# Gate and up products with x's sums stationary, the weights moving 512 columns wide, and the activations turned by TensorE

## The chip, the cores and the metric

The kernel runs on one core of one Trainium2 chip. The time is device microseconds of one launch; a smaller number is better. All arithmetic is float32: each operand is split into a rounded part (float32r, called hi or wh) and the rest (lo or wl), and one product is three matmuls: hi by hi, hi by lo, lo by hi.

## The reference

Two layers, each with a feed-forward block (FFN), a mixing part (latent attention beside a causal convolution) and a second FFN, on 512 tokens of width 1024. Only the FFNs are changed:

```
def swiglu(x, w_gate, w_up, w_down):
    return (jax.nn.silu(x @ w_gate) * (x @ w_up)) @ w_down
for l in range(DEPTH):                 # 2
    x = x + 0.5 * swiglu(rms_norm(x, ffn1_norm[l]), ...)   # 1024 -> 2816 -> 1024
    ...                                                    # mixing part
    x = x + 0.5 * swiglu(rms_norm(x, ffn2_norm[l]), ...)
    x = rms_norm(x, post_norm[l])
```

There are so four FFNs: FFN1 and FFN2 of layers 0 and 1. The hidden width 2816 is 22 blocks of 128.

## The kernel before

x lies transposed in SBUF: 8 blocks m of 128 features by 512 tokens. The gate and up products of an FFN are computed by a pair of hidden blocks p (128 gate and 128 up columns each, twice).

The first two pairs are plain (`plain`): 8 blocks of features, 512 tokens moving, the weights stationary; this starts before the norm is known, since the norm's factor R is multiplied on afterwards (`plain_out`, L255 to L260). The other nine pairs (`pair`) use a scheme of seven products in place of eight. The product is cut in two along features, tokens and hidden columns; each quarter product has 4 blocks of features, and with the three matmuls and gate beside up that makes 24 matmuls. Sums of the weights' quarters (`s1` to `s4`, L336 to L339) are made on VectorE for each pair, sums of x's quarters (`operands`: `b11`, `b21`, `b22`, `t1` to `t4`) once for an FFN. In these products the weights are stationary and half of the tokens, 256 columns, move. `product` issues the matmuls, `split_into` (L223, L225) splits each weight tile on ScalarE (hi) and VectorE (lo).

The down products (`group`, L140 to L142, updates of x at L399) follow in four chunks of hidden blocks (`CHUNKS`). TensorE's results lie as hidden columns by tokens, as the down product needs its moving operand.

The norm: `Stats` squares x on ScalarE (L172), adds up on GpSimd (L173) and sums over features by a matmul with ones (L178); GpSimd takes the power (L158); `spread` (L192, L196) makes of the factor for each token a tile R with all partitions alike.

The order on each engine is set by a list scheduler: an instruction written earlier goes first if its operands and buffers are ready by the scheduler's own estimate, else a later one goes ahead. Buffers come from pools: 7 PSUM banks (`ps`), 41 slots `r` for split x and activations, 4 each for weights `wh` and `wl`, 3 `raw`, 5 `fr`.

Of the kernel before, what the change touches and what calls it, by code (L numbers as in the profile page):

```python
# [15 lines left out]
P = 128  # L16
# [19 lines left out]
RING = 41  # L36
CHUNKS = ((0, 2), (2, 5), (5, 8), (8, 11))
# [30 lines left out]
def encoder_kernel(ctx: ExitStack, tc: tile.TileContext, xT, consts, vecs, rgain, wgu1, wd1,  # L68
# [56 lines left out]
    def load_w(src, w, kind=""):  # L125
        raw = wpool.tile([P, WC], FP, tag="raw", name=nm("raw"), bufs=3)
        nc.sync.dma_start(out=raw[:, :w], in_=src)
# [100 lines left out]
    def ffn(l, gx, norm, wgu, wd, gain, done, w0=None):  # L228
        with tc.tile_pool(name="f", bufs=4) as fpool:
            ffn_body(fpool, l, gx, norm, wgu, wd, gain, done, w0)  # L230

    def ffn_body(fpool, l, gx, norm, wgu, wd, gain, done, w0):

        def wide(tag="e"):
            return fpool.tile([P, 2, S], FP, tag=tag, name=nm(tag))

        def raw(q, p):
            t = fpool.tile([P, WC], FP, tag="fr", name=nm("fr"), bufs=5)
            nc.sync.dma_start(out=t, in_=wgu[l, p, q])
            return t

        def plain(os, ws, ks):
            for gu, o in enumerate(os):
                for k in ks:
                    w = ws[k % 2]
                    c = slice(gu * 512 + k // 2 * P, gu * 512 + (k // 2 + 1) * P)  # L250
                    mm3(o, w[0][:, c], w[1][:, c], gx[k][0], gx[k][1], k == 0, k == KD - 1)

        def plain_out(os, R):
            t = tmp()
            V.tensor_tensor(t, os[0], R, ALU.mult)  # L255
            s = tmp()
            A.activation(s, t, AF.Silu)
            u = tmp()
            V.tensor_tensor(u, os[1], R, ALU.mult)
            V.tensor_tensor(u, u, s, ALU.mult)  # L260
            return split(u)

        X = {n: [] for n in ("b11", "b21", "b22", "t1", "t2", "t3", "t4")}

        def operands(R):

            es, od = [], []
            for i in range(2):
                e, o = wide(), wide()
                for j in range(2):  # L270
                    for par, t in ((0, e), (1, o)):
                        m = 4 * i + 2 * j + par
                        V.scalar_tensor_tensor(t[:, j], x[:, m, :], gain[:, m:m + 1], R, ALU.mult, ALU.mult)
                        yield
                es.append(e)
                od.append(o)
            yield "x"

            def halved(src):
                hi, lo = slot(FR), slot(FR)  # L280
                h3, l3 = (v.rearrange("p (j t) -> p j t", j=2) for v in (hi, lo))
                A.copy(h3, src)
                V.tensor_tensor(l3, src, h3.bitcast(FP), ALU.subtract)  # L283
                return hi, lo

            def diff(a, b, op=ALU.subtract):
                t = tmp().rearrange("p (j t) -> p j t", j=2)
                V.tensor_tensor(t, a, b, op)  # L288
                return t
            for n in ("b11", "b21"):  # L290
                for i in range(2):
                    X[n].append(halved((es if n == "b11" else od)[i][:, :, 0:HS]))
                    yield
            for i in range(2):
                b11, b12, b21, b22 = (v[i][:, :, h * HS:(h + 1) * HS] for v in (es, od) for h in range(2))
                t3 = diff(b12, b22)
                yield
                t2 = diff(t3, b11)
                yield
                X["t2"].append(halved(t2))  # L300
                yield
                X["t3"].append(halved(t3))
                yield
                t1 = diff(b11, b12)
                yield
                X["t1"].append(halved(t1))
                yield
                t4 = diff(b21, t2, ALU.add)
                yield
                X["t4"].append(halved(t4))  # L310
                yield
                X["b22"].append(halved(b22))
                yield

        def product(o, w, n, start, stop):
            for gu in range(2):
                for k in range(4):
                    hi, lo = X[n][k // 2]
                    t = slice(k % 2 * HS, (k % 2 + 1) * HS)
                    c = slice(gu * 512 + k * P, gu * 512 + (k + 1) * P)  # L320
                    mm3(o[:, gu * HS:(gu + 1) * HS], w[0][:, c], w[1][:, c], hi[:, t], lo[:, t],
                        start and gu == 0 and k == 0, stop and k == 3, True)

        def copied(o, src):
            A.copy(o, src)
            return o

        def pair(p):

            a11, a12, a21, a22 = (raw(q, p) for q in range(4))  # L330
            s3 = wpool.tile([P, WC], FP, tag="raw", name=nm("raw"), bufs=3)
            bx, by, bz = bank(), bank(), bank()
            product(bx, split_into("a11", a11), "b11", True, True)
# [603 lines left out]
```

## Time and profile before

| what | value |
|---|---|
| median of 3 runs | 1858.15 us (1855.42 to 1858.24) |
| span of the profiled execution | 1857.6 us |
| TensorE matmul busy | 1816.5 us (98%) |
| TensorE weight load busy | 1623.6 us (87%) |
| VectorE busy | 1353.9 us (73%) |
| ScalarE busy | 935.7 us (50%) |
| GpSimd busy | 341.5 us (18%) |
| bytes moved by DMA | 175.72 MB, mean 95 GB/s |

The profiled execution has no time of its own beside its span; the span is 0.55 us under the median of the runs. Busy time of matmuls is of modelled, overlapping records: what one matmul takes of TensorE is the distance of its start from the next one's start. The same holds for VectorE, where each instruction's record reaches some 0.08 us into the next one.

### The profile page before, as it was taken

The numbers are of one execution on the slowest core, as the hardware profiler recorded it, in microseconds if no ns is written. First come the engines' busy times: TensorE is split into PE (matmuls) and PEld (weight loads), VectorE is DVE, ScalarE is ACT, GpSimd is POOL, SyncE is SP. The second block draws the span as 40 slices with busy tenths as digits, with TensorE's granted clock in tenths as the row PEclk, the third lists the DMA queues.
The fourth block names the chain that finished last, engine by engine and source line by source line (L and its number), as shares of the span: only waits on it lengthen the run. The fifth ranks groups of instructions, "written<-read, shape, count | busy, mean of one in ns | idle before, by whom it ended". The sixth has DMA issues, their size and how long they took to land.

```text
span 1857.6 us, 27862 instructions
## 1 busy us (share of the span) xinstructions
PE 1816.5 (98%) x11240; PEld 1623.6 (87%) x11240; DVE 1353.9 (73%) x1761; ACT 935.7 (50%) x1467; POOL 341.5 (18%) x242
## 2 busy tenths in 40 slices
PE   7999999999899999999999999999999999999997
PEld 6898989888688898989888999898978788989895
DVE  5985858678855985858679767675989569767674
ACT  4453535457944453535634535354679435535351
POOL 3000000238924000000310000002589310000002
PEclk9999999999999999999999999999999999999998
DMA  6142422424213142423512414123250322424221
GB/s 217 41 142 69 135 68 91 122 74 125 46 58 110 39 140 77 128 77 94 165 54 63 150 55 148 57 87 114 78 148 1 108 80 63 142 63 143 63 86 63
DMA packets 55569, 175.72 MB, mean 95 GB/s; under 512 B 6160, under 2 KB 6544, under 8 KB 55440
## 3 DMA queue, kind: packets, MB, share of 16 engines
q1 hardware_dynamic: 53856, 169.37, 29.3%
q0 software_dynamic: 1152, 4.19, 1.3%
q8 instruction: 88, 1.44, 0.3%
q10 hardware_dynamic: 432, 0.38, 0.1%
q14 instruction: 41, 0.34, 0.1%
HBM read 171.82 MB, written 2.10 MB: 94 GB/s over the span
## 4 chain that ended last, share of the span: by engine, by line
PE 82%; DVE 7%; POOL 4%; ACT 4%; issue 3%; DMA 0%; POOLq 0%; ACTq 0%; DVEq 0%
PE ps L140 26%; PE ps L142 26%; PE ps L141 25%; PE ps L664 2%; PE ps L630 1%; ACT pr L707 1%; POOL y L711 1%; DVE wl L135 1%; POOL acc L173 1%; DVE r L283 1%; PE ps L651 1%; DVE cv L703 1%; DVE t L288 1%; POOL sck L158 1%; ACT wh L129 1%
## 5 line engine op out<-in xcount | busy, mean ns | idle before, releaser
L141 PE MATMUL ps<-r,wh 128*128 128x256 f32 (+1 forms) x3280 | 1060.7, 325 | 2.3 <-DVE r L153 2.2
L140 PE MATMUL ps<-r,wh 128*128 128x256 f32 (+1 forms) x3280 | 1053.7, 328 | 8.9 <-ACT wh L129 7.9
L142 PE MATMUL ps<-r,wl 128*128 128x256 f32 (+1 forms) x3280 | 1052.7, 325 | 3.9 <-DVE wl L135 1.9
L140 PEld LDWEIGHTS ps<-r,wh 128*128 128x128 f32 x3280 | 621.4, 191 | 64.8 <-ACT wh L129 8.7
L141 PEld LDWEIGHTS ps<-r,wh 128*128 128x128 f32 x3280 | 625.8, 191 | 55.1 <-DVE r L153 3.2
L142 PEld LDWEIGHTS ps<-r,wl 128*128 128x128 f32 x3280 | 622.2, 191 | 56.8 <-DVE wl L135 4.4
L223 ACT CAST wh<-fr 128x1024 fp32r<-128x1024 f32 x216 | 226.9, 1051 | 318.1 <-PE ps L141 233.0
L129 ACT CAST wh<-raw 128x768 fp32r<-128x768 f32 (+4 forms) x214 | 187.7, 883 | 337.5 <-PE ps L141 170.0
L173 POOL TENSOR_TENSOR acc<-acc,t 128x512 f32<-128x512 f32 x52 | 89.4, 1725 | 1308.5 <-ACT t L172 1307.4
L225 DVE TENSOR_TENSOR wl<-fr,wh 128x1024 fp32r<-128x1024 f32 x216 | 263.8, 1222 | 79.6 <-ACT wh L223 76.6
L135 DVE TENSOR_TENSOR wl<-raw,wh 128x768 fp32r<-128x768 f32 (+4 forms) x198 | 209.5, 1063 | 125.9 <-ACT wh L129 124.5
L399 DVE SCALAR_TENSOR_TENSOR x<-ps,x 128x512 f32<-128x512 f32 x128 | 87.6, 687 | 119.1 <-PE ps L142 119.1
L711 POOL TENSOR_TENSOR y<-y,pr 128x509 f32<-128x509 f32 (+15 forms) x120 | 157.5, 1313 | 51.9 <-ACT pr L707 44.6
L703 DVE SCALAR_TENSOR_TENSOR cv<-r,vec,cv 128x511 f32<-128x511 f32 (+14 forms) x120 | 87.7, 731 | 3.1 <-ACT cv L699 1.7
L707 ACT ACTIVATE pr<-r,vec 128x511 f32<-128x511 f32 (+14 forms) x120 | 83.5, 722 | 8.2 <-POOL y L711 8.0
L223 ACT CAST wh<-raw 128x1024 fp32r<-128x1024 f32 x36 | 37.7, 1047 | 70.3 <-PE ps L141 70.3
L146 ACT CAST r<-t 128x512 fp32r<-128x512 f32 x96 | 55.7, 620 | 33.5 <-DVE t L260 20.6
L147 DVE TENSOR_TENSOR r<-t,r 128x512 fp32r<-128x512 f32 x96 | 64.7, 686 | 10.2 <-ACT r L146 10.2
L225 DVE TENSOR_TENSOR wl<-raw,wh 128x1024 fp32r<-128x1024 f32 x36 | 44.1, 1225 | 30.9 <-ACT wh L223 30.9
L630 PE MATMUL ps<-r,r 96*128 96x384 f32 (+3 forms) x128 | 47.8, 492 | 8.6 <-ACT r L609 4.4
L336 DVE TENSOR_TENSOR raw<-fr,fr 128x1024 f32<-128x1024 f32 x36 | 44.0, 1223 | 12.9 <-DMA fr<-in_wgu 12.9
L153 DVE SCALAR_TENSOR_TENSOR r<-x,vec,r 128x512 fp32r<-128x512 f32 x40 | 45.9, 1148 | 10.2 <-ACT r L152 10.2
(165 smaller groups left out, 1596.4 us busy)
## 6 DMA issues: line engine op xcount, KB each, us to landing
fr<-in_wgu SPq DMA_DIRECT2D x144, 512.0 KB, 3.6
raw<-in_wd SPq DMA_DIRECT2D x96, 384.0 KB, 3.1
raw<-in_wgu SPq DMA_DIRECT2D x32, 512.0 KB, 3.5
raw<-in_wd SPq DMA_DIRECT2D x32, 256.0 KB, 2.6
raw<-in_wcv SPq DMA_DIRECT2D x16, 512.0 KB, 3.6
raw<-in_wout SPq DMA_DIRECT2D x16, 512.0 KB, 4.5
wl<-in_wout POOLq DMA_DIRECT2D x8, 512.0 KB, 6.7
raw<-in_wql SPq DMA_DIRECT2D x6, 512.0 KB, 3.5
```

The costliest lines, as they stand in the source:

```text
L129: A.copy(hi[:, :w], raw[:, :w])
L135: (G if kind in POOLW.split() else V).tensor_tensor(lo[:, :w], raw[:, :w], hi[:, :w].bitcast(FP), ALU.subtract)
L140: T.matmul(o, lh, rh, start=first, stop=False, skip_group_check=free)
L141: T.matmul(o, lh, rl, start=False, stop=False, skip_group_check=free)
L142: T.matmul(o, ll, rh, start=False, stop=last, skip_group_check=free)
L173: (eng or (V if last else G)).tensor_tensor(self.acc, self.acc, sq, ALU.add)
L223: A.copy(hi[:, :w], src[:, :w])
L225: V.tensor_tensor(lo[:, :w], src[:, :w], hi[:, :w].bitcast(FP), ALU.subtract)
L399: V.scalar_tensor_tensor(x[:, m, :], pd, 0.5, x[:, m, :], ALU.mult, ALU.add)
L703: V.scalar_tensor_tensor(acc[:, s:], u[c][:, :S - s], tap(k), acc[:, s:], ALU.mult, ALU.add)
L707: A.activation(pr[:, s:], u[c][:, :S - s], AF.Copy, scale=tap(k))
L711: order["conv"] = G.tensor_tensor(acc[:, s:], acc[:, s:], pr[:, s:], ALU.add).ins
```

## The change

All 22 hidden blocks now go by the scheme of seven products, in six units of 4, 4, 4, 4, 4 and 2 blocks. In a product a 128-token slice of x's sum is stationary and the weights move, 512 columns wide (gate and up of 4 half blocks), in the last unit 256. The result has tokens on partitions. So the norm's factor is a number for each partition (`gated`, no R is needed in an FFN), and the activations are turned by TensorE (`turned`: 4 transposes of 128 by 128 into a bank) before they are split and used by the down products. x's sums are made without the norm, from x times the gain: `block(m)` makes `b11`, `b21` and `b22` as each block of x is finished, and `sums` makes `t1` to `t4` during the first unit, called by `advance`. The down products of unit u are issued between the products of unit u+1 (`down`, two feature blocks for each load of weights); those of the last two units come after all products. At the start of the program x's blocks are loaded in the order 0, 2, 4, 6, 1, 3, 5, 7 among the first weight tiles. After the second FFN of layer 0, x is no longer scaled in place by ScalarE: `post` multiplies gain and factor together on VectorE. Pools: 9 `fr` buffers, 40 slots; the scratch of GpSimd's DMAs is set to 4096 bytes.

```
+UNITS = (4, 4, 4, 4, 4, 2)
...
+    class Operands:
...
+        def block(self, m):
+            g, q = self.g[:, m:m + 1], m // 2
+            if m % 2:
+                hi, lo = split_scaled(x[:, m, :], g)
+                for n, c in (("b21", slice(0, HS)), ("b22", slice(HS, S))):
+                    self.k[n][q] = hi[:, c], lo[:, c]
+                return
...
+            A.activation(hi, x[:, m, 0:HS], AF.Copy, scale=g)
+            V.scalar_tensor_tensor(lo, x[:, m, 0:HS], g, hi.bitcast(FP), ALU.mult, ALU.subtract)
+            self.k["b11"][q] = hi, lo
...
+        def scaled(self, i, par, half, b, op):
+            out = slot()
+            for j in range(2):
+                m, c = 4 * i + 2 * j + par, slice(j * HS, (j + 1) * HS)
+                V.scalar_tensor_tensor(out[:, c], x[:, m, half * HS:(half + 1) * HS], self.g[:, m:m + 1],
+                                       b[:, c], ALU.mult, op)
+            return out
...
+        def product(o, ts, n, start, stop):
+            w = [split_into("q", t) for t in ts]
+            kn = 4 // len(w)
+            N = WC // kn
+            order = [(j, k) for j in range(2) for k in range(4)]
...
+            for j, k in order:
+                hi, lo = ops.k[n][k]
+                t = slice(j * P, (j + 1) * P)
+                c = slice(k % kn * N, (k % kn + 1) * N)
+                mm3(o[j][:, :N], hi[:, t], lo[:, t], w[k // kn][0][:, c], w[k // kn][1][:, c],
+                    start and k == 0, stop and k == 3, True)
...
+        def gated(t, src, out, N):
+            h = N // 2
+            for j in range(2):
+                r = rt[0][:, 2 * t + j:2 * t + j + 1]
+                A.activation(out[j][:, :h], src[j][:, :h], AF.Silu, scale=r)
+                V.scalar_tensor_tensor(out[j][:, :h], src[j][:, h:N], r, out[j][:, :h], ALU.mult, ALU.mult)
+            return out
...
+        def turned(vs, N, act):
+            for b in range(2):
+                for i in range(N // 2 // P):
+                    ps = bank()
+                    for t in range(2):
+                        for j in range(2):
+                            T.transpose(ps[:, (2 * t + j) * P:(2 * t + j + 1) * P],
+                                        vs[b][t][j][:, i * P:(i + 1) * P], ident)
+                    act.append(split(ps))
...
+        def unit(u, between):
+            a11, a12, a21, a22 = (quarter(u, q) for q in range(4))
...
+            product(bx, a11, "b11", True, True)
+            a = sides(copied(bx, N))
+            between(0)
+            product(by, a12, "b21", True, True)
+            if first:
+                ops.advance(6)
+            add(s3, a11, a21)
+            add(a21, a21, a22)
+            add(a11, a11, a21)
+            between(1)
+            if first:
+                rt.append(norm())
+            join(a, a, by, ALU.add, N)
+            gated(0, a, a, N)
+            product(bx, a11, "t2", False, True)
...
+            product(bx, a12, "b22", False, True)
...
+        for ms in ((0, 1, 2), (3,), (4,), (5,), (6,), (7,)):
+            ws = [load_w(wd[l, m, :, f0:f0 + n * P], n * P) for m in ms]
+            pds = [bank() for _ in ms]
+            for pd, w in zip(pds, ws):
+                group(pd, w, acts, range(n0), n)
+            if ms[0] == 0:
+                turned(vs, UNITS[-1] * P, acts)
+            for m, pd, w in zip(ms, pds, ws):
+                group(pd, w, acts, range(n0, n), n)
+                update(m, pd)
+                done(m)
```

In `unit`, `between(0)` is where the turned activations of the unit before are written, `between(1)` to `between(4)` where two feature blocks each of its down products are; the products with `t3`, `t1` and `t4` left out here follow the one with `t2` in the same way. In the changed kernel the lines are others: L146 to L148 are the three matmuls, L366 the transposes, L231 `split_into`'s lo, L323 the weights' sums, L268 `scaled`, L159 `split_scaled`'s lo, L179 the norm's sum, L347 `join`, L357 `gated`.

The first place is VectorE at the program's start, around the last addition of the norm's sum of squares (`acc`). Before, the lo parts of x (`r`) and weights (`wl`) stand around it:

```order
L135 TENSOR_TENSOR wl_236<-raw_232,wh_234 128x1024
L153 SCALAR_TENSOR_TENSOR r_139<-x,vec,r_138 128x512
L173 TENSOR_TENSOR acc_147<-acc_147,t_167 128x512
L135 TENSOR_TENSOR wl_242<-raw_238,wh_240 128x1024
L153 SCALAR_TENSOR_TENSOR r_144<-x,vec,r_143 128x512
L184 TENSOR_SCALAR vtok_223<-ps_224 128x4
L192 TENSOR_TENSOR t_294<-cst,rtok_230 128x512
```

Now x's sums (L268) and five of the weights' sums (L323) stand behind the same addition, and ahead of the third product:

```order
L323 TENSOR_TENSOR fr_165<-fr_165,fr_169 128x1024
L179 TENSOR_TENSOR acc_142<-acc_142,t_162 128x512
L268 SCALAR_TENSOR_TENSOR r_249<-x,vec,r_246 128x256 x2
L323 TENSOR_TENSOR fr_167<-fr_167,fr_171 128x1024
L323 TENSOR_TENSOR fr_106<-fr_106,fr_165 128x1024
L347 TENSOR_TENSOR e_209<-e_209,ps_212 128x512
L347 TENSOR_TENSOR e_209<-e_209,ps_213 128x512
L268 SCALAR_TENSOR_TENSOR r_252<-x,vec,r_249 128x256 x2
L268 SCALAR_TENSOR_TENSOR r_258<-x,vec,r_255 128x256
L190 TENSOR_SCALAR vtok_278<-ps_279 128x4
```

What waits for the norm's sum on this in-order engine has grown from the rest of two plain blocks to the operands of the third product.

The second place is TensorE at the end of a product. Before, in FFN1 of layer 0, 256 tokens move and the weights (`wh`, `wl`, named last) are stationary:

```order
L140 MATMUL ps_721<-r_469,wh_724 128x256
L141 MATMUL ps_721<-r_470,wh_724 128x256
L142 MATMUL ps_721<-r_469,wl_726 128x256
L140 MATMUL ps_721<-r_473,wh_724 128x256
L141 MATMUL ps_721<-r_474,wh_724 128x256
```

Now, at the first product of the second unit of FFN2 of layer 0, the weights move 512 wide, x's parts (`r`) are stationary, and the transposes of the activations (`t`, `e`) follow:

```order
L146 MATMUL ps_5418<-wh_5423,r_4943 128x512
L147 MATMUL ps_5418<-wl_5425,r_4943 128x512
L148 MATMUL ps_5418<-wh_5423,r_4944 128x512
L366 MATMUL ps_5454<-cst,t_5394 128x128
L366 MATMUL ps_5463<-cst,e_5092 128x128 x2
L366 MATMUL ps_5463<-cst,t_5394 128x128
L366 MATMUL ps_5454<-cst,t_5394 128x128
L366 MATMUL ps_5463<-cst,t_5394 128x128
L146 MATMUL ps_5417<-wh_5570,r_5147 128x512
```

The transposes stand in runs of one to sixteen between products or inside them.

The third place is VectorE in the first unit of FFN2 of layer 0, near its end. Before, that stretch holds what comes out of the plain blocks (L255 to L260) and the first sums of x (L288):

```order
L259 TENSOR_TENSOR t_5896<-ps_5831,R_5794 128x512
L288 TENSOR_TENSOR t_5981<-e_5880,e_5881 128x512
L147 TENSOR_TENSOR r_5815<-t_5811,r_5814 128x512
L260 TENSOR_TENSOR t_5896<-t_5896,t_5894 128x512
L288 TENSOR_TENSOR t_5983<-t_5981,e_5880 128x512
```

Now the last operand of `t4` (`r_5321`) and the weights of the next unit (`wl_5421`) stand behind sums of the next unit's weights:

```order
L323 TENSOR_TENSOR raw_5416<-fr_5401,fr_5409 128x1024
L231 TENSOR_TENSOR wl_5364<-fr_5044,wh_5362 128x1024
L347 TENSOR_TENSOR e_5253<-e_5253,ps_5058 128x512
L347 TENSOR_TENSOR e_5253<-e_5253,ps_5059 128x512
L323 TENSOR_TENSOR fr_5407<-fr_5407,fr_5411 128x1024
L231 TENSOR_TENSOR wl_5368<-fr_5046,wh_5366 128x1024
L159 SCALAR_TENSOR_TENSOR r_5321<-r_5317,r_5320 128x512
L231 TENSOR_TENSOR wl_5421<-fr_5399,wh_5419 128x1024
```

The operands of seven products are made in the unit that uses them, where before two plain pairs and a chunk of down products stood ahead of the first use.

More of the change, by code (lines that the diff above doesn't have):

```diff
@@ L35 @@
 HS = S // 2
-RING = 41
-CHUNKS = ((0, 2), (2, 5), (5, 8), (8, 11))
+UNITS = (4, 4, 4, 4, 4, 2)
+TILES = tuple(u // 2 for u in UNITS)
+FIRST = tuple(4 * sum(TILES[:i]) for i in range(len(UNITS)))
+FRB = 9
+RING = 40
+WIDE = 4
 CONV = "DAAD"
@@ L849, in done3 @@
                 st3.add(x[:, m, :], last=m == KD - 1)
-            ffn(l, gx, norm2, wgu2, wd2, vv(l, "g2"), done3)
+            ffn(l, ops, norm2, wgu2, wd2, done3)
             ps = spread(st3.token(D))
```

375 lines of the change are left out of this document (180 added, 195 removed).

## The prediction

> **What bounds the kernel now.** I read the page first, then groups with shapes kept apart, stretches of time, and the timeline where a duration had to be settled.
>
> ```profile
> span 1857.6 us, 27862 instructions
> PE 1816.5 (98%) x11240; PEld 1623.6 (87%) x11240; DVE 1353.9 (73%) x1761; ACT 935.7 (50%) x1467; POOL 341.5 (18%) x242
> PEclk9999999999999999999999999999999999999998
> PE 82%; DVE 7%; POOL 4%; ACT 4%; issue 3%; DMA 0%; POOLq 0%; ACTq 0%; DVEq 0%
> ```
>
> TensorE is the bound: 98% busy at full clock, and 82% of the chain that ended last. So each nanosecond of matmul pitch (start to next start) counts, as long as the others keep feeding it. The stretches show where it isn't fed:
>
> ```profile
> core 0: us, PE busy (x) PEld busy (x) DVE busy (x) ACT busy (x) POOL busy (x), PEclk, DMA share, GB/s
> 0.00:10.00 10.00, 2.14 (x5) 1.76 (x6) 3.69 (x14) 5.65 (x8) 3.11 (x10) 1.00 0.84 305
> 10.00:20.00 10.00, 9.54 (x34) 6.87 (x33) 6.12 (x6) 8.63 (x14) 9.69 (x8) 1.00 1.03 409
> 0.00:45.00 45.00, 34.78 (x127) 27.08 (x128) 23.02 (x35) 21.21 (x28) 16.66 (x19) 0.92 0.62 224
> 45.00:385.00 340.00, 339.56 (x2207) 310.84 (x2206) 247.08 (x298) 157.18 (x221) 12.08 (x7) 1.00 0.31 94
> 484.00:531.00 47.00, 45.38 (x351) 39.20 (x352) 38.39 (x76) 36.58 (x92) 35.91 (x29) 1.00 0.01 1
> 985.00:1020.00 35.00, 32.31 (x206) 29.37 (x205) 31.61 (x39) 16.09 (x22) 0.00 (x0) 0.95 0.23 68
> ```
>
> Within the FFN from 45 to 385 us TensorE rests 0.44 us in 340. Only the opening (10.2 us idle, clock 0.92) and the start of layer 1 (2.7 us idle, clock 0.95) lose anything. The change lives in the FFNs: it can win only by less TensorE work, and lose only by new waits.
>
> **TensorE's work.** An FFN had 1512 matmuls of 256 columns and 192 of 512 for gate and up; it gets 840 of 512 and 168 of 256. Over four FFNs 5376 narrow ones go and 2592 wide ones come. Their busy times (283 and 391 ns) overlap, so I take pitches from stretches with one shape only:
>
> ```profile
> L141 PE MATMUL ps<-r,wh 128*128 128x256 f32 x2016 | 567.0, 283 | 0.0
> L141 PE MATMUL ps<-r,wh 128*128 128x512 f32 x1264 | 494.2, 391 | 2.3 <-DVE r L153 2.2
> ...
> core 0: us, PE busy (x), PEclk, DMA share, GB/s
> 180.00:230.00 50.00, 50.00 (x417) 1.00 0.42 129
> 243.00:271.00 28.00, 28.00 (x125) 1.00 0.10 30
> ```
>
> A stretch counts records that reach into it, so (50 + 0.28)/417 gives 120.5 ns and (28 + 0.39)/125 gives 227 ns. Two narrow ones cost 241, one wide one 227. The change of matmuls is 2592 x 0.227 - 5376 x 0.1205 = 588.4 - 647.8 = -59.4 us: about 22 from columns no longer computed (two plain pairs go to seven products), the rest from 14 ns saved on each pair.
>
> The Trainium skill, TensorE: Matmul & The Clock Gate, Back-to-back issue gap, has another price: columns at full clock plus 2.5 ns, so 109 and 216 ns as an estimate by its formula, and the matmuls would save 28 us instead of 59. The stretches above disagree with it for these float32r streams.
>
> **Transposes.** 88 in an FFN, 352 in all, that were not there. The same form runs in attention (x10), and the latent keys have pairs of it between other matmuls:
>
> ```profile
> 489.72 1.29 PE L651 MATMUL ps<-cst,r 128*128 128x128 f32 x10
> 490.84 2.34 PE L664 MATMUL ps<-r,r 128*128 128x64 f32 x20
> ...
> 423.00 0.33 PE L141 MATMUL ps<-wl,r 128*128 128x384 f32 x1
> 423.17 0.34 PE L142 MATMUL ps<-wh,r 128*128 128x384 f32 x1
> 423.34 0.38 PE L509 MATMUL ps<-cst,ck 128*128 128x128 f32 x2
> 423.48 0.42 PE L140 MATMUL ps<-wh,r 128*128 128x384 f32 x1
> 423.74 0.33 PE L141 MATMUL ps<-wl,r 128*128 128x384 f32 x1
> ```
>
> Ten take 1.12 us, 112 ns each. Around a pair, 423.17 to 423.74 is 0.57; less two pitches of 0.173 that leaves 0.224, again 112 each. 352 x 0.112 = +39 us; both rows are of the added form, so the ends are close (38 to 41).
>
> **R.** Four of ten spreads over tokens go (the FFNs scale by partition).
>
> ```profile
> L196 PE MATMUL ps<-t,ones 128*128 128x512 f32 x20 | 11.1, 646 | 2.1 <-DVE t L192 2.1
> ```
>
> They can't be worth more than 4/10 of 11.1 us; records overlap, so half: -2 us (-4 to 0). TensorE's sum is -59 + 39 - 2 = -22 us.
>
> **VectorE, as the feeder.** Back to back, its instructions also follow each other faster than they last:
>
> ```profile
> 985.90 0.68 DVE L399 SCALAR_TENSOR_TENSOR x<-ps,x 128x512 f32<-128x512 f32 x1
> 986.50 0.68 DVE L135 TENSOR_TENSOR wl<-raw,wh 128x512 fp32r<-128x512 f32 x1
> ...
> 1003.55 1.22 DVE L339 TENSOR_TENSOR fr<-fr,fr 128x1024 f32<-128x1024 f32 x1
> 1004.68 1.22 DVE L225 TENSOR_TENSOR wl<-fr,wh 128x1024 fp32r<-128x1024 f32 x1
> ...
> 42.24 5.38 DVE L273 SCALAR_TENSOR_TENSOR e<-x,vec,R 128x512 f32<-128x512 f32 x8
> 47.54 0.68 DVE L259 TENSOR_TENSOR t<-ps,R 128x512 f32<-128x512 f32 x1
> ...
> 192.61 0.42 DVE L355 TENSOR_TENSOR t<-t,t 128x256 f32<-128x256 f32 x1
> 192.95 1.22 DVE L338 TENSOR_TENSOR fr<-fr,fr 128x1024 f32<-128x1024 f32 x1
> ```
>
> So 0.60 us for 512 elements, 1.13 for 1024, 0.66 for 512 with a scale by partition (5.30/8), 0.34 for 256, and by the same 0.06 more an estimate of 0.40 for 256 with a scale.
>
> A steady unit of 4 blocks: VectorE has 14 splits, 8 weight sums and 4 down splits of 1024 (29.4), 6 joins, 4 activation splits, 8 updates of x (10.8) and 8 gates (3.2): 43.4 us. TensorE has 168 + 96 wide matmuls and 16 transposes: 61.7 us. At 70% VectorE stays ahead, as before; ScalarE has less. I put +1 us (0 to 4) on all steady units. The last unit is half as wide: TensorE 22 us, VectorE about 19, still covered, and 36 matmuls of down products cover its last activations. GpSimd's four accumulating loads and the convolution keep their order.
>
> **First units.** Here x's sums are made in the unit that uses them, with no down products beside it: the cover of 43.6 us of plain matmuls (192 x 0.227) and 8 x 12 down matmuls is gone. In FFN2 of layer 0 I added VectorE's rows in their order, from the last lo part that the first product needs to the second weight tile of the next unit: 20 of 1024, 9 of 512 with scale, 6 without, 21 of 256 with scale, which is 22.6 + 5.9 + 3.6 + 8.4 = 40.5 us. TensorE has 180 wide matmuls and the norm's sum in the same stretch, about 42 us. VectorE keeps up by one or two microseconds, so I put +1 on each FFN2 (0 to 7 if rows cost what they last, 0.08 more each, or if GpSimd slows them, below). In FFN1 of layer 1 eight multiplications of x (5.3 us) come on top, and the norm there takes two powers of GpSimd one after the other: by the same addition TensorE waits some 5 us, where before it lost 2.7 idle and 0.05 x 35 to the clock. +1 (-3 to +6).
>
> **The opening.**
>
> ```profile
> 7.86 0.79 PE L140 MATMUL ps<-r,wh 128*128 128x512 f32 x1 [7.86 <-ACT wh L129]
> 21.84 0.51 PE L141 MATMUL ps<-r,wh 128*128 128x512 f32 x1 [2.25 <-DVE r L153]
> ...
> L173 POOL TENSOR_TENSOR acc<-acc,t 128x512 f32<-128x512 f32 x6 | 10.2, 1702 | 0.4
> ...
> 22.95 0.69 DVE L173 TENSOR_TENSOR acc<-acc,t 128x512 f32<-128x512 f32 x1 [1.17 <-POOL acc L173]
> ...
> L153 DVE SCALAR_TENSOR_TENSOR r<-x,vec,r 128x512 fp32r<-128x512 f32 x40 | 45.9, 1148 | 10.2 <-ACT r L152 10.2
> ```
>
> GpSimd's six additions set the norm's sum at 22.95 before, and will again. Behind it VectorE now has, up to the third product's last operand, 9 rows of 1024, 8 of 256 with scale, two joins, two lo parts and two gates: 10.2 + 3.2 + 1.2 + 1.3 + 0.8 = 16.7 us, so that operand comes at 40.3. Data is no later: x and the first unit's weights are 6.3 MB, and 7.1 MB had landed at 20 us on the same queue. Of the first four products (96 matmuls, 21.8 us) some 28 are left at 40.3, which ends them at 46.7; the loss is 46.7 - 21.8 - 1 = 24 us. Before, 117 matmuls of 0.227 and 1.5 us of sums and spread in 45 us lose 17. +7 (2 to 13).
>
> **Sum.** -22 + 1 + 1 + 1 + 1 + 7 = -11 us, against the span of 1857.6 and thus 1847 for the median of 1858.15.
>
> **Rivals.**
> - A, the feeders are faster than that: ScalarE and VectorE work ahead during down products and mixing, and the opening's stalls overlap the half clock. The opening then adds 2 and the first units nothing: -20 us, 1838. For it: in 45 to 385 us nothing was lost. Against: the order puts the sums behind the norm's.
> - B, part of the gain is lost: the opening at +13, first units at +2 to +3 each: about -3, 1855 to 1861, no change.
> - C, VectorE's queue in the four first units decides, slower. L153 lasts 1148 ns on average against the 0.66 us pitch of L273's like rows: GpSimd's norm additions run beside just these rows. If the 9 such rows lose 0.4 us each and the 48 others 0.08, a first unit loses some 7 us; three of them with the opening at +13 and steady units at +4 make -22 + 13 + 21 + 4 = +16, 1874. It turns the sign once waits exceed 22 us in all.
> - D, wide moving saves no time beyond the columns: -22 instead of -59, so +26 us, 1884. The two stretches speak against it.
> - E, transposes let the clock drop. Half clock for 5% of 35 us cost 1.75 us at the start of layer 1; once in each of 24 units is +42, 1889. Against: from 484 to 531 us runs of ten alternate with small matmuls at clock 1.00. The Trainium skill, the same page, Part 4: PE-mode transpose, says that transposes do not count as activity for the clock gate; by that rule E is possible, but here each unit mixes 1.8 us of them with 60 us of matmuls.
>
> **How the numbers follow.** Forecast 0.43 (1843 to 1854), A 0.22, B 0.16, C 0.13, D 0.03, E 0.03. About 0.2% (3.7 us) can be told from no change. Faster: forecast and A, 0.65; same: B, 0.17 with a little of C; slower 0.18. The range leaves out D, E and most of C: 1836 to 1862. The likeliest case's own range is 1843 to 1854.
>
> **What would show it.** Matmuls 512 wide at 227 ns in the products, 352 transposes at about 112; TensorE idle in 0 to 45 us about 7 us more, with waits for VectorE's x sums (L268, L159) there; under 3 us lost in each first unit of FFN2; none in steady units. Wrong if the pitch of wide products is above 232, if steady units wait for `wl` of L231, or if the clock drops outside first units.

## Result and the profile after

The changed kernel takes 1881.09 us (median of four runs, 1880.24 to 1882.26) against 1858.06 of the kernel before, measured beside it: a ratio of 1.0128 (95% interval 1.0114 to 1.0143), slower by 23 us. Forecast were 1847 and a gain. Below, each run stands beside the kernel before as measured with it; e2, e3, e4, b2, e6, f4, e7, e9 and e10 are one run each, and the old kernel's own runs lie between 1854.4 and 1861.3 us, so two or three microseconds of a single run say nothing.

The page of the changed kernel, with the lines that answer to those shown of before:

```profile
span 1880.5 us, 22843 instructions
PE 1806.5 (96%) x8800; PEld 1507.7 (80%) x8800; DVE 1427.0 (76%) x1861; ACT 965.3 (51%) x1507; POOL 348.3 (19%) x242
PEclk8999999999999999999989999999999999999998
PE 78%; DVE 10%; ACT 4%; issue 4%; POOL 2%; DMA 1%; SPq 0%; POOLq 0%; DVEq 0%; ACTq 0%
```

TensorE has 10 us less of modelled work, but a longer span. The stretches of the changed kernel say where it rests (columns as in the prediction):

```profile
core 0: us, PE busy (x) PEld busy (x) DVE busy (x) ACT busy (x) POOL busy (x), PEclk, DMA share, GB/s
0.00:45.00 45.00, 26.19 (x77) 18.31 (x77) 36.32 (x51) 25.51 (x39) 19.98 (x19) 0.81 0.49 183
45.00:385.00 340.00, 338.17 (x1609) 283.75 (x1608) 248.45 (x298) 159.24 (x219) 10.09 (x6) 0.99 0.30 96
560.00:610.00 50.00, 44.80 (x184) 35.69 (x183) 47.03 (x49) 24.98 (x38) 24.47 (x11) 0.93 0.19 71
925.00:975.00 50.00, 35.52 (x143) 27.57 (x142) 49.67 (x59) 26.95 (x43) 23.25 (x14) 0.83 0.11 38
1020.00:1310.00 290.00, 290.00 (x1396) 244.24 (x1395) 205.27 (x242) 132.61 (x182) 10.08 (x6) 1.00 0.29 93
1495.00:1535.00 40.00, 34.97 (x144) 28.08 (x143) 40.00 (x41) 17.27 (x27) 16.96 (x9) 0.91 0.08 27
```

And the same entries (an entry is where an FFN starts) of the kernel before (FFN2 of layer 0, the end of FFN2 with the start of FFN1 of layer 1, FFN2 of layer 1):

```profile
553.00:603.00 50.00, 49.75 (x222) 40.65 (x221) 28.30 (x27) 22.25 (x29) 23.97 (x11) 1.00 0.32 101
910.00:960.00 50.00, 50.00 (x227) 40.94 (x226) 38.08 (x42) 27.19 (x40) 23.86 (x14) 1.00 0.34 100
1445.00:1485.00 40.00, 39.58 (x176) 31.56 (x175) 25.20 (x31) 21.23 (x32) 17.01 (x8) 1.00 0.35 115
```

Read the VectorE column. In the first units of the changed kernel it is busy 47 of 50, 49.7 of 50 and 40 of 40 us, where it was 28, 38 and 25 of the same; and TensorE, which hardly rested there, rests 5 to 14 us at a lower clock. From 1020 to 1310, in steady units, TensorE is busy all the time at clock 1.00. Of the waits in the entry of FFN1 of layer 1 the answer names the operands:

```profile
PE ps L148 <- DVE wl L141: 7.0, 1, 7.0
PE ps L146 <- ACT r L158: 5.6, 1, 5.6
PE ps L147 <- DVE wl L231: 1.3, 1, 1.3
```

For all kernels I worked out TensorE's loss by stage from the trace: over all matmuls, the distance to the next start less the undisturbed distance of that width (227 ns for 512 columns, 120 for 256, 109 for a transpose). It holds waits and slow clock together. The stages are 0 to 50 us and 95 to 120 us around each other FFN's entry; the last column is all other stages.

| kernel | us | opening | FFN2, layer 0 | FFN1, layer 1 | FFN2, layer 1 | rest |
|---|---|---|---|---|---|---|
| before | 1858.06 | 9.3 | 3.7 | 5.8 | 3.5 | 26.7 |
| changed | 1881.09 | 20.3 | 12.0 | 21.4 | 11.9 | 26.8 |
| b2, before, additions out | 1848.77 | 1.9 | 3.5 | 4.3 | 3.5 | 26.1 |
| e1, additions on VectorE | 1874.73 | 17.3 | 11.4 | 19.8 | 11.8 | 23.9 |
| e2, additions out | 1849.16 | 15.7 | 4.7 | 10.1 | 4.8 | 24.5 |
| e3, x's sums out | 1856.35 | 19.4 | 6.3 | 11.0 | 7.3 | 20.9 |
| e4, both out | 1827.33 | 10.8 | 3.1 | 1.2 | 3.1 | 19.3 |
| e9, all on VectorE | 1870.85 | 17.2 | 9.4 | 20.8 | 9.9 | 23.8 |
| f9, plain first units | 1851.80 | 1.7 | 3.1 | 10.3 | 3.1 | 20.5 |
| e10, f9 with additions out | 1841.00 | 1.6 | 3.1 | 1.1 | 3.1 | 19.6 |

The four first units lose 65.6 us in place of 22.3: 43 us more. That is the sign of the result.

### The profile page after: what moved, and what is told of

It is laid out like the page before. It is cut to its first block, busy times and chain, and to the rows that moved or that the text cites. A ratio compares the mean times of both kernels' runs of the same rounds, so it can differ in the third digit from the quotient of the medians.

```text
span 1880.5 us, 22843 instructions
## 1 busy us (share of the span) xinstructions
PE 1806.5 (96%) x8800; PEld 1507.7 (80%) x8800; DVE 1427.0 (76%) x1861; ACT 965.3 (51%) x1507; POOL 348.3 (19%) x242
## 4 chain that ended last, share of the span: by engine, by line
PE 78%; DVE 10%; ACT 4%; issue 4%; POOL 2%; DMA 1%; SPq 0%; POOLq 0%; DVEq 0%; ACTq 0%
PE ps L148 24%; PE ps L146 24%; PE ps L147 24%; DVE fr L323 2%; PE ps L366 2%; PE ps L718 2%; DVE wl L231 2%; PE ps L684 1%; ACT pr L761 1%; POOL y L765 1%; PE ps L705 1%; DVE raw L323 1%; DMA fr<-in_wgu 1%; DVE r L268 1%; DVE cv L757 1%
## 5 line engine op out<-in xcount | busy, mean ns | idle before, releaser
L146 PE MATMUL ps<-wh,r 128*128 128x512 f32 (+3 forms) x1488 | 546.8, 375 | 30.2 <-ACT r L158 14.2
L147 PE MATMUL ps<-wl,r 128*128 128x512 f32 (+3 forms) x1488 | 553.5, 374 | 8.2 <-DVE wl L231 8.2
L148 PE MATMUL ps<-wh,r 128*128 128x512 f32 (+3 forms) x1488 | 548.2, 373 | 1.1 <-DVE r L159 0.9
L148 PE MATMUL ps<-r,wl 128*128 128x512 f32 x1008 | 391.3, 390 | 7.5 <-DVE wl L141 7.0
L147 PE MATMUL ps<-r,wh 128*128 128x512 f32 x1008 | 392.3, 390 | 0.0
L146 PE MATMUL ps<-r,wh 128*128 128x512 f32 x1008 | 390.7, 393 | 0.3 <-ACT r L152 0.3
L231 DVE TENSOR_TENSOR wl<-fr,wh 128x1024 fp32r<-128x1024 f32 x264 | 324.3, 1229 | 82.8 <-ACT wh L229 81.8
L146 PEld LDWEIGHTS ps<-wh,r 128*128 128x128 f32 x1488 | 284.1, 191 | 79.1 <-ACT r L158 16.1
L179 POOL TENSOR_TENSOR acc<-acc,t 128x512 f32<-128x512 f32 x52 | 90.9, 1754 | 1304.3 <-ACT t L178 1303.3
L147 PEld LDWEIGHTS ps<-wl,r 128*128 128x128 f32 x1488 | 284.3, 191 | 57.3 <-DVE wl L231 11.0
L148 PEld LDWEIGHTS ps<-wh,r 128*128 128x128 f32 x1488 | 284.0, 191 | 49.4 <-DVE r L159 3.5
L148 PEld LDWEIGHTS ps<-r,wl 128*128 128x128 f32 x1008 | 189.6, 188 | 48.4 <-DVE wl L141 7.4
L146 PEld LDWEIGHTS ps<-r,wh 128*128 128x128 f32 x1008 | 189.5, 188 | 41.7 <-ACT r L152 1.2
L147 PEld LDWEIGHTS ps<-r,wh 128*128 128x128 f32 x1008 | 189.6, 188 | 40.2 <-issue 1.4
L141 DVE TENSOR_TENSOR wl<-raw,wh 128x1024 fp32r<-128x1024 f32 (+3 forms) x134 | 161.2, 1204 | 63.0 <-ACT wh L135 62.1
L419 DVE SCALAR_TENSOR_TENSOR x<-ps,x 128x512 f32<-128x512 f32 x160 | 109.5, 686 | 104.4 <-PE ps L148 104.3
L323 DVE TENSOR_TENSOR fr<-fr,fr 128x1024 f32<-128x1024 f32 x132 | 169.7, 1294 | 17.6 <-DMA fr<-in_wgu 17.5
```

Of the source, the lines that this page charges most:

```text
L141: (G if kind in POOLW.split() else V).tensor_tensor(lo[:, :w], raw[:, :w], hi[:, :w].bitcast(FP), ALU.subtract)
L146: T.matmul(o, lh, rh, start=first, stop=False, skip_group_check=free)
L147: T.matmul(o, lh, rl, start=False, stop=False, skip_group_check=free)
L148: T.matmul(o, ll, rh, start=False, stop=last, skip_group_check=free)
L179: (eng or (V if last else G)).tensor_tensor(self.acc, self.acc, sq, ALU.add)
L231: V.tensor_tensor(lo[:, :w], src[:, :w], hi[:, :w].bitcast(FP), ALU.subtract)
```

## Experiments

**Theories.** In the changed kernel VectorE rows stand beside GpSimd's work that last two to three times what they should:

```profile
562.48 7.52 POOL L141 TENSOR_TENSOR wl<-raw,wh 128x1024 fp32r<-128x1024 f32 x3 [15.13 <-PE ps L147]
569.96 2.27 POOL L179 TENSOR_TENSOR acc<-acc,t 128x512 f32<-128x512 f32 x1
...
567.65 3.43 DVE L323 TENSOR_TENSOR raw<-fr,fr 128x1024 f32<-128x1024 f32 x1
571.00 1.78 DVE L159 SCALAR_TENSOR_TENSOR r<-x,vec,r 128x512 fp32r<-128x512 f32 x1
...
579.97 0.67 DVE L814 TENSOR_TENSOR x<-x,ps 128x512 f32<-128x512 f32 x1
580.57 1.21 DVE L231 TENSOR_TENSOR wl<-fr,wh 128x1024 fp32r<-128x1024 f32 x1
581.71 1.21 DVE L323 TENSOR_TENSOR fr<-fr,fr 128x1024 f32<-128x1024 f32 x1
```

A sum of weights (L323) takes 3.43 us beside GpSimd and 1.21 without. So the first theory was contention. The second: VectorE has too much work of its own in a first unit, x's sums above all.

**e1, e2, e3.** e1 and e2 edit `Stats.add`, e3 `Operands.advance` (the three edits in one listing, marked at the right, some lines joined):

```
-            (eng or (V if last else G)).tensor_tensor(self.acc, self.acc, sq, ALU.add)
+            V.tensor_tensor(self.acc, self.acc, sq, ALU.add)                      # e1
+            if eng or last: V.tensor_tensor(self.acc, self.acc, sq, ALU.add)      # e2
 
-            for _ in range(n): next(self.steps, None)
+            for a, b in (("t1", "b11"), ("t2", "b21"), ("t3", "b22"), ("t4", "b11")):   # e3
+                self.k[a] = self.k[b]
```

> Edit: the additions of the squares (L179), which six of eight times (and twelve of sixteen after FFN2 of layer 0) run on GpSimd, all run on VectorE. First theory (contention): VectorE's rows that last 2 to 3.9 us in place of 1.2 beside these additions are what delays the splits that TensorE waits for in the first units; VectorE gets 6 x 0.6 = 3.6 us of work for each norm, and loses 10 to 14 us of stretched rows; the first units of FFN2 lose 3 to 5 us in place of 12, that of FFN1 of layer 1 7 to 11 in place of 21, the opening 14 to 18 in place of 20: 1853 to 1863 us in all. Second theory (VectorE has too much to do in its own right, x's sums above all): VectorE's work grows by 18 us over the five norms, and the time stays or rises: 1878 to 1895.

> Left out of the computation: six of each norm's seven additions of squares (all on GpSimd), so the norm is of two blocks of features; nothing else of the order of work is taken away. It gives the whole price of GpSimd's additions with nothing put on VectorE. Contention: no row of VectorE over 1.4 us in the first units, these lose 2 to 4 us each, FFN1 of layer 1 5 to 9: 1850 to 1858 us. Second theory: 1876 to 1881, since VectorE's own work is the same.

> Left out of the computation: x's sums and their splits (L268, L278 and the splits of the four sums); the five products that need them take plain quarters of x. Second theory (x's sums on VectorE decide): VectorE is rid of 16 x 0.40 + 8 x 0.60 = 11 us in each first unit, these lose 2 to 4 us, FFN1 of layer 1 some 8, the opening 13: 1848 to 1856 us. Contention: only the waits behind the norm's sum go (about 3 us in FFN2's, 6 in FFN1's, 7 in the opening's first unit), those ahead of it stay, 2 to 7 us each: 1860 to 1868.

Measured: e1 1874.73 (before 1856.75, ratio 1.0092, 1.0075 to 1.0109), e2 1849.16, e3 1856.35. At its ratio to the kernel before, the changed kernel would take 1880.5 here; so each theory has a large effect when its work is taken away (31 and 24 us). In e1 both theories' forecasts missed, contention's by 12 us and the second's by 3 from the other side: moved from GpSimd to VectorE, the additions gave back 6 of the 31 us. In e2 the opening keeps 15.7 us and FFN1 of layer 1 10.1.

**e4, b2, e6, f1.** e4 is e2 and e3 together; b2 is e2's edit in the old kernel; e6 empties `post`; f1 lets DMAs add (two lines joined):

```
-            (eng or (V if last else G)).tensor_tensor(self.acc, self.acc, sq, ALU.add)
+            if eng or last: V.tensor_tensor(self.acc, self.acc, sq, ALU.add)
+            else: G.dma_start(out=self.acc, in_=sq, accum_op=ALU.add)             # f1
```

> Left out of the computation: both what e2 left out (six of seven additions of squares) and what e3 left out (x's sums). The two alone took off 31 and 24 us. If VectorE is simply full in the first units, each us taken from it is worth one until it has slack; the opening and FFN1 of layer 1 still have some to gain after e2 (15.7 and 10.1 us of waits and slow clock), the two FFN2 entries hardly (4.7 each against 3.6 before the change): 1835 to 1843. If the two are separate causes with waits of their own, they add up: 1824 to 1828.

> The kernel before the change, with the same additions of squares left out of the computation. If its plain pairs leave VectorE enough time in spite of GpSimd's additions, only the opening's wait for the norm's sum and FFN1 of layer 1 gain: 1850 to 1856 against 1857. If contention cost the old kernel as much as the new one, 1825 to 1835, and contention then explains nothing of the difference.

> Changed kernel; left out of the computation: the eight multiplications of x by layer 0's post norm (L911, 5.3 us of VectorE in FFN1 of layer 1) and their spread. If VectorE is full there until the end of the unit, FFN1's first unit loses 15 to 18 us in place of 21: 1874 to 1877. If these rows lie behind the waits (they stand at 977 to 990 us, the waits at 934 to 974), nothing changes there: 1879 to 1882.

> Full computation: the additions that GpSimd made are DMAs that add the square to the sum in SBUF (accumulating, issued by GpSimd's queue). If GpSimd's reads of SBUF beside rows of VectorE with two SBUF operands are the cause, these rows last 1.2 us again and VectorE gets no work for it: as e2, plus what the chain of DMAs delays the norm (some 3 us each, a block of x comes every 4 to 5 us in FFN2, faster in the opening): 1850 to 1862. If the DMAs are late, or their descriptors block as the additions did: 1865 to 1890.

Measured: e4 1827.33, b2 1848.77, e6 1878.18, f1 1886.61 (ratio 1.0152, 1.0131 to 1.0174). e4 is 54 us under the changed kernel (1881.1 here), and e2 and e3 alone take off 31 and 24. By what was written ahead that is the answer of two separate causes (1824 to 1828); one full engine was forecast at 1835 to 1843, and missed. But by stage (table) the two do not add up: they take 8.9 and 8.8 us off the FFN2 entries, where alone they take off 13.0 and 11.7 and the floor is the old kernel's loss, and 9.5 off the opening, where alone they take off 5.5. The total near the sum is thus partly chance, and e4 settles neither theory. e4 is also 21.4 us under b2, the old kernel without the same additions (it makes x's sums, behind plain pairs); as the two lose nearly the same in all stages together (37.5 and 39.3 us), this is about what the change's matmuls are worth. b2 came out lower than expected; nearly all of it is the opening (9.3 to 1.9), while the FFN2 entries move by 0.2. GpSimd's additions cost the old kernel 8.5 us, the changed one 31. Without the post norm's rows (e6, between its two forecasts) FFN1's entry loses 19.6 in place of 21.4. f1 relieves FFN2 (5.3 and 7.1 in the place of 12), but other norms now end late: TensorE has a new wait, for sums that a chain of DMAs delivers (0.86 us of GpSimd's queue and 3.3 us to landing each).

```profile
PE ps L187 <- DVE acc L180: 27.2, 6, 9.8
```

**f2 to f5.** f2 sums the squares on TensorE (`Rows`: a 512-wide matmul against a column of ones for each block, then four small ones that turn the row into columns; `lh` is the column of ones); f3 makes the opening's first unit plain, f5 that of FFN1 of layer 1 too, f4 only the opening's, without f2. `plain` takes a quarter of the weights against both halves of the tokens.

```
+            A.activation(sq, src, AF.Square, scale=scale)
+            T.matmul(self.ps[0:self.n, :], lh, sq, start=self.count == 1, stop=self.count == self.n * KD)
...
+        def plain_unit():
+            a11, a12, a21, a22 = (quarter(0, q) for q in range(4))
...
+            plain(o, a11, ("b11", "b12"), True, False)
+            plain(o, a12, ("b21", "b22"), False, True)
...
+            ops.advance(4)
...
-            nvs = unit(u, between)
+            nvs = plain_unit() if u == 0 and ops.full else unit(u, between)
```

> Full computation: in the five norms that a first unit waits for (the opening, both FFN2, and the two sums of FFN1 of layer 1) the squares go to TensorE as a moving operand 512 wide against a column of ones, eight matmuls to a norm, 40 in all, 9 us at 0.227; neither GpSimd nor VectorE adds. If GpSimd's additions beside VectorE are the larger cause, the first units come out as in e2 (opening 16, FFN2 5 each, FFN1 of layer 1 10 us of waits and slow clock), and the time is e2's 1849 plus 9 for the matmuls and 2 for the norms that keep their additions: 1854 to 1862. If the matmuls fill waits that are there anyway, 1850 to 1854. If TensorE's wait for squares is a new stall, over 1866.

> f2, and the first unit of the opening plain: eight products of raw quarters in place of seven, 24 matmuls (5.4 us) more, no sums of weights or of x ahead of the second unit (x's sums are made during it). The old kernel without additions lost 1.9 us in its plain opening, e2 15.7. If making x's sums and weights' sums in the very unit that needs them is the second cause, the opening loses 2 to 4 us in place of 16, and the time is f2's less 12 to 14 plus 5.4: 6 to 9 us under f2, 1846 to 1852. If data or the scalar engine set the opening, 0 to 5 us over f2.

> f3, and the first unit of FFN1 of layer 1 plain too. There e2 lost 10.1 us and the old kernel without additions 4.3, so 5.8 is to be had for 5.4 us of matmuls: within 2 us of f3. If its waits came of the two sums of squares alone, 5 us over f3.

> The changed kernel with only the opening's first unit plain, GpSimd's additions as they were. The old kernel's opening lost 9.3 us, the changed one's 20.3; a plain one here loses some 8 to 10 and costs 5.4 of matmuls: 1873 to 1877. If contention alone made the opening slow, 1881 to 1886.

Measured: f2 1862.61 (ratio 1.0032, 1.0018 to 1.0046), f3 1858.37 (1.0009, 0.9997 to 1.0022), f5 1861.96 (1.0025, 1.0015 to 1.0035), f4 1867.22. f4 says most: the plain opening loses 1.6 us in place of 20.3 with GpSimd's additions as they were, so contention alone did not make the opening slow; the rows for the sums, which this unit takes out of VectorE's queue, did. Its forecast was 8 to 10 us lost, and so missed by 6 us on the good side. f2 is 0.6 us above its range, f3 6 above, and f5 3.6 above f3 where at most 2 was expected. f2's own matmuls wait for squares that aren't there yet, in f3 6.7 us (1.7, 2.2 and 2.8 at the three later entries), and TensorE waits up to 2.9 us for a part of x at the FFN2 entries; the forecasts had both at nothing.

**f6, e7, e9, f8, b3.** f6 is f3 with each row matmul one block later; e7, e9 and f8 move the splits of the output weights from GpSimd to VectorE in the changed kernel, e1 and f3; b3 is the old kernel with f2's `Rows`.

```
-            T.matmul(self.ps[0:self.n, :], lh, sq, start=self.count == 1, stop=self.count == self.n * KD)
+            self.wait.append((lh, sq))
+            if last:
+                self.flush(len(self.wait))
+            elif len(self.wait) > LATER * self.n:
+                self.flush(1)
...
-POOLW = "wo"
+POOLW = ""
```

> f3, with each block's squares summed by TensorE one block later (the last one at once), since in f3 TensorE waited 1.7, 2.2 and 2.8 us for squares in the three later entries. If those waits were the placing, they go and 4 to 7 us come off f3: 1848 to 1854, faster than both kernels. If the matmuls only meet the next late operand, the same waits stand at L150 or L151 and the time stays: 1855 to 1859.

> The changed kernel with its four splits of output weights in each mixing part (L141 on GpSimd, 10 us in all at each entry of FFN2) on VectorE; GpSimd's additions stay. If these splits stretch VectorE's rows as the additions do (two rows of 3.4 and 1.5 us stand beside them even in e2), VectorE wins about what it takes on (4 x 1.13), and the FFN2 entries lose 9 to 12 us as before: 1876 to 1882. If the splits are the larger part of the contention there, the entries lose 5 to 7: 1868 to 1872.

> e1 and e7 together: all additions of squares and the splits of output weights on VectorE, so GpSimd reads no SBUF beside the first units. No row of VectorE is stretched then, and what is left is VectorE's own work. If its being full is what counts, whoever fills it, the FFN2 entries still lose 8 to 11 us and FFN1 of layer 1 16 to 20: 1868 to 1876. If stretching is worse than the same work in its own queue, the entries fall to 4 to 6: 1856 to 1864.

> f3 with the splits of output weights on VectorE too: there VectorE has 15 us of slack at the FFN2 entries. If GpSimd's splits make x's updates late there (TensorE waited 2.9 and 2 us for x's parts and squares at each), 3 to 8 us come off f3: 1849 to 1855, under both kernels. If not, within 2 us of f3, 1856 to 1860.

> The kernel before the change, with the squares of the same five norms summed by TensorE as in f2. Its own loss to GpSimd's additions was 10 us (without them 1849, one run), the matmuls cost 9, the norms that keep additions 1: 1854 to 1860, no faster than it was. Then f3 and this one are equal, and relief alone does not make the change pay. If the matmuls hide in the opening's waits, 1848 to 1852.

Measured: f6 1857.46 (0.9995, 0.9986 to 1.0005), e7 1875.32, e9 1870.85, f8 1861.71 (1.0017, 1.0007 to 1.0027), b3 1883.18 (1.0135, 1.012 to 1.015). f6 came out at the second of its forecasts and f8 above both of its own: neither wait was the placing or the splits. e7 fell between its two, 6 us under the changed kernel. b3 missed by 23 us: of the 23 between its span (1880.7) and the old kernel's, 40 matmuls are 9.1, waits for squares 6.7, and other losses grow by 6.9; f2's cure is no cure of the old kernel. e9 is the clean test of contention, and came out as forecast for a full VectorE (1868 to 1876): GpSimd neither adds nor splits at the entries, no row of VectorE is stretched there, and the first units still lose 57 us. Its stretches in the opening and FFN2 of layer 0:

```profile
0.00:45.00 45.00, 27.30 (x93) 19.84 (x94) 38.45 (x62) 27.69 (x43) 7.10 (x13) 0.89 0.49 184
557.00:607.00 50.00, 45.47 (x196) 37.20 (x195) 46.48 (x66) 29.34 (x45) 1.18 (x1) 0.93 0.17 60
```

GpSimd has 1.18 us there, VectorE is as full as before (46.5 of 50), and TensorE waits. So the cause is that VectorE's queue in the first units delivers TensorE's operands too late; contention is one of the things that lengthen this queue, not a separate stall, and without it 10 us are gained. No run keeps VectorE's rows and changes only their order, so how much is amount and how much order stays open.

**f9 and e10.** f9 makes all four first units plain, in a full computation; e10 is f9 with e2's edit.

```
-        ops, st = Operands(g), Stats()
+        ops, st = Operands(g, True), Stats()
...
-            nops = Operands(gc)
+            nops = Operands(gc, True)
```

> The changed kernel with all four first units plain (eight products of raw quarters, x's sums made meanwhile); GpSimd's additions and splits as they were. It costs 4 x 24 x 0.227 = 21.8 us of matmuls and takes from VectorE, in each first unit, six splits and eight sums of 1024 (16 us). If VectorE being full there is the cause, the first units lose what the old kernel's did or less (opening 1.6 as in f4, FFN2 4 each, FFN1 of layer 1 6, in place of 20, 12, 12 and 21): 1880 - 50 + 22 = 1852, 1848 to 1858. If the entries are late for another reason (x's updates, the norm), they keep 8 to 15 us each: 1870 to 1885.

> The same kernel, with six of each norm's seven additions of squares left out of the computation (as in e2). Where VectorE has room, GpSimd's additions cost nothing: 0 to 4 us under it. If they cost TensorE by themselves, 20 to 30 under it, as they did in the changed kernel.

Measured: f9 1851.80 against 1857.36, ratio 0.9968 (0.9956 to 0.998): faster than both kernels, as forecast. e10 1841.00, which missed (0 to 4 expected, 11 found). The opening of f9, its FFN2 stretch, where GpSimd still has 19 us of additions and splits, and FFN1 of layer 1 in e4:

```profile
0.00:45.00 45.00, 36.51 (x158) 30.26 (x159) 36.10 (x51) 28.49 (x43) 19.65 (x19) 1.00 0.71 265
550.00:600.00 50.00, 50.00 (x227) 41.48 (x226) 36.35 (x40) 23.58 (x36) 19.10 (x10) 1.00 0.29 98
...
900.00:950.00 50.00, 50.00 (x228) 41.31 (x227) 46.02 (x59) 32.55 (x47) 2.93 (x2) 1.00 0.34 118
```

In its FFN2 stretch f9's VectorE has 14 us of room and TensorE never rests. But the busy share by itself decides nothing: f9's opening has as much VectorE work in its 45 us as the changed kernel's (36.1 and 36.3) and loses 1.7 us in place of 20.3, and in e4 VectorE is busy 46 of 50 us while TensorE never rests. What counts is which rows stand ahead of the operand that TensorE needs next.

e10's gain lies in one place, FFN1 of layer 1 (10.3 to 1.1). Two sums of squares make twelve additions there; beside them VectorE is busy 19.7 of the 20 us from 900 to 920 in f9 and comes to x's sums at 927.28, 7.7 us later than in e10 (919.61). So here it had no room, and GpSimd's additions cost 9.2 us, near the 11.3 of the changed kernel (e2). Being late, it then runs the post norm's eight rows ahead of a split that TensorE waits 5.8 us for (in e10 the same rows in the same order end 7.3 us earlier, and that wait is 0.3 us):

```profile
970.11 5.38 DVE L950 SCALAR_TENSOR_TENSOR x<-x,vec,R 128x512 f32<-128x512 f32 x8
975.41 1.22 DVE L328 TENSOR_TENSOR fr<-fr,fr 128x1024 f32<-128x1024 f32 x1
976.54 1.22 DVE L141 TENSOR_TENSOR wl<-raw,wh 128x1024 fp32r<-128x1024 f32 x1
977.68 1.22 DVE L231 TENSOR_TENSOR wl<-fr,wh 128x1024 fp32r<-128x1024 f32 x1
```

```profile
PE ps L147 <- DVE wl L231: 5.8, 1, 5.8
```

The first listing is VectorE's timeline, the second TensorE's waits. Writing that post norm into the second unit is the next step that this points to; it was not tried.

## Why the prediction was wrong, point by point

- **Matmuls, -59.4: right.** In a run of wide products thirteen distances lie between the starts at 130.84 and 133.78, 226 ns each, and the count is 2592 more and 5376 fewer. The sum over all widths at undisturbed distances is 1602.1 us in place of 1661.0, -58.9. Rival D is out. The other price, by the formula of the Trainium skill, TensorE: Matmul & The Clock Gate, Back-to-back issue gap, is out too (216 ns against 226 here); that section gives the formula for a single matmul by itself, which the prediction doesn't say.

```profile
130.84 0.39 PE L147 MATMUL ps<-wl,r 128*128 128x512 f32 x1
...
133.78 0.39 PE L148 MATMUL ps<-wh,r 128*128 128x512 f32 x1
...
138.94 0.27 PE L366 MATMUL ps<-cst,e 128*128 128x128 f32 x1
...
139.81 0.93 PE L366 MATMUL ps<-cst,e 128*128 128x128 f32 x7
```

- **Transposes, +39: right.** Eight in (139.81 - 138.94), 109 ns each; all 352 take 38.0.
- **Spreads, -2: right** (their distances sum to 3.3 in place of 5.5). TensorE's sum of -22 is thus confirmed by these (-23.1), and e4 against b2 (-21.4) agrees.
- **Steady units, +1: right.** The four FFNs past their entries lose about 7 us before and after.
- **First units of FFN2, +1 each: this step failed.** They cost 8.3 and 8.4 more. The prediction added up VectorE's rows from the last lo part on, at undisturbed pitches, and found 40.5 us against 42 of TensorE. But VectorE was not at rest when that stretch began. Weight sums (L323), which the plain pairs did not have, stand in its queue ahead of x's updates and x's parts; beside GpSimd's additions and splits they last 2.3 to 3.4 us; so each update, and each x part behind it, came late. In FFN2 of layer 0 TensorE rests 2.3 us for a part of x (L254), which waits for x's update (L814), which stands behind a stretched weight sum:

```profile
587.51 1.53 POOL L179 TENSOR_TENSOR acc<-acc,t 128x512 f32<-128x512 f32 x1 [3.44 <-ACT t L178]
...
587.81 2.31 DVE L323 TENSOR_TENSOR fr<-fr,fr 128x1024 f32<-128x1024 f32 x1
...
590.04 0.68 DVE L814 TENSOR_TENSOR x<-x,ps 128x512 f32<-128x512 f32 x1
...
590.75 0.51 ACT L254 ACTIVATE r<-x,vec 128x256 fp32r<-128x256 f32 x1 [2.45 <-DVE x L814]
```

```profile
PE ps L146 <- ACT r L254: 2.3, 1, 2.3
```

With GpSimd's additions out (e2, one run) the two entries lose 4.7 and 4.8, that is 1.0 and 1.3 more than before: the forecast's +1. So the sum of rows held where they are mostly undisturbed, and what failed is that the forecast put GpSimd's work beside them at nothing. A margin of 1.5 us in 40 is no margin where the row with the stretched L153 (1148 ns) was already on the page. It was given to rival C at 0.13.
- **FFN1 of layer 1, +1: same step, 15.6 more.** It has twelve additions of squares beside its weight sums, and a down product waits 7.0 us for its own split (`wl`, L141) behind them. The terms that the prediction did name there weigh less: without the post norm's rows the unit gains 2 us (e6).
- **Opening, +7 (2 to 13): +11, and the first matmul 0.7 later.** Right in sign and within its bounds, in part by luck: VectorE's queue did set it, but not the norm's sum behind GpSimd, from which the forecast was worked out. e2 took only 4.6 us off, the plain opening (f4) 18.7.
- **Sum.** -58.9 + 38.0 - 2.2 + 43.3 + 0.7 = +21, of 22.9 between the two spans; 2 us isn't placed.
- **Rivals.** C is what happened: waits in the first units, past its own point of 22 us in all. It gave 1874, since it had some 7 us for each of the three later first units, where FFN1's took 15.6. E in the form given (transposes) is out, at clock 1.00 from 1020 to 1310 us. In the FFNs past their first units the granted clock fell only once, from 77.44 to 80.85 us, behind two waits of 1.0 and 0.9 us. But a clock term is there: around the longer waits of the first units the granted clock is 0.5 for 3.4 to 10.2 us at a time, and the matmuls that start in it lose about 16 us in place of about 4.5 before. After the 7 us wait (clock 0.5 from 937.59 to 944.42) four distances take 1.70 us, 425 ns each:

```profile
941.46 0.79 PE L148 MATMUL ps<-r,wl 128*128 128x512 f32 x1 [7.01 <-DVE wl L141]
942.05 0.63 PE L146 MATMUL ps<-r,wh 128*128 128x512 f32 x1
...
943.75 0.63 PE L147 MATMUL ps<-r,wh 128*128 128x512 f32 x1
```

## What to carry to other kernels

When a change takes cover away from a stage, add up what the feeding engine is asked for in that stage from the moment its queue last stood empty, with the stretched durations that it shows beside its neighbours, up to the operand that the bound engine needs next. The busy share of the feeder alone is a poor measure: in FFN2 of layer 0 94% went with 12.0 us lost, 91% (e2) with 4.7 and 73% (f9) with 3.1, but in FFN1 of layer 1 92% (e4) went with 1.2. Moving work between two engines that stand beside each other gained 6 us (e1), 6 (e7) and 10 (e9), taking the additions away 31 (e2); so try the two largest sources together, and read the answer by stage. Operands made from a late result (sums of x) belong in the unit after the first, beside a first unit that needs only raw parts: f9, which takes the sums of weights out of the first units too, pays 22 us of matmuls and loses 47 us less there.

## What the runs showed of the hardware

A VectorE row with both tensors in SBUF is stretched beside GpSimd's additions by about 1.1 us (the shortest of these additions lasted 1.28): in the changed kernel 128 x 1024 sums of weights that ran wholly beside L179 lasted 2302 ns on average (x4) against 1218 (x156), x's lo parts 1767 (x7) against 702 (x36). Rows with one tensor in PSUM are not: x's updates (L419) took 677 beside it and 687 without. In the same few microseconds:

```profile
932.33 1.51 DVE L255 SCALAR_TENSOR_TENSOR r<-x,gc,r 128x256 fp32r<-128x256 f32 x1
933.76 0.68 DVE L419 SCALAR_TENSOR_TENSOR x<-ps,x 128x512 f32<-128x512 f32 x1
934.36 3.90 DVE L323 TENSOR_TENSOR fr<-fr,fr 128x1024 f32<-128x1024 f32 x2
```

The Trainium skill, SBUF — State Buffer, Who interferes with whom, says that a VectorE instruction with two SBUF inputs contends with a GpSimd instruction that reads SBUF, and that one with at most one SBUF input, outside the two-port modes, doesn't. The trace agrees (2302 against 1218, 677 against 687). The price stood in the trace before: there x's lo parts (L153) lasted 1776 ns wholly beside GpSimd's additions (x12) and 741 with no GpSimd work beside them (x14), about 1.04 us more, where rival C took 0.4.
